# The first branch's products move into the second attention; four more gates become pairs of seven products

## The chip, the cores and the metric

The kernel runs on one core of a Trainium2 chip. The metric is device time in microseconds (us) of one execution. The core's engines are TensorE (PE; PEld is its weight load), VectorE (DVE), ScalarE (ACT), GpSimd (POOL) and SyncE (SP), which issues most DMAs. Each engine works through its own queue in a fixed order and waits on semaphores of the others.

## The reference

One layer of a decoder trunk with 1024 positions and 1024 channels, in float32. Two attentions work on the same normalised input; each goes through a projection (a branch), is weighted by a sigmoid gate, and the sum is mixed and added to x. A gated MLP with a causal convolution follows.

```python
xn = rmsnorm(x, norm_mix_w[l])
proj = xn @ w_in[l]
da_q, da_k, da_v, sw_q, sw_k, sw_v, g_da, g_sw = split_cols(proj)
y_da = diff_attention(da_q, da_k, da_v, lam, lam_init, subln_w[l])     # 4 heads of 128
y_sw = sliding_window_attention(sw_q, sw_k, sw_v, sinks[l])            # 8 heads of 64, window 128
merged = jax.nn.sigmoid(g_da) * (y_da @ w_br_da[l]) + jax.nn.sigmoid(g_sw) * (y_sw @ w_br_sw[l])
x = x + merged @ w_mix_out[l]
x = x + conv_ffn(rmsnorm(x, norm_ffn_w[l]), w_up[l], conv_w[l], conv_b[l], w_down[l])
return rmsnorm(x, norm_final_w)
```

The projection has 34 column blocks of 128: 0 to 17 are the attentions' operands, 18 to 25 the gates of the first branch, 26 to 33 those of the second.

## The kernel before, in words

Activations lie transposed, channels on the 128 partitions and the 1024 positions along the free axis, in halves of 512. Each float32 operand is kept as a high part (a rounded cast, ACT) and a low part (the rest, a subtraction), and each product is three matmuls: high by high, high by low, low by high (`mm3`, lines 146 to 155, and `product`, line 879). A column block with 1024 input rows is 8 x 3 x 2 = 48 matmuls of 512 columns.

**Projections** (`project`). x is split into `xh` and `xl`, eight tiles each, and stays in the chip. Blocks 0, 4, 8, 18 and 20 (`plain`) are computed with 48 matmuls each. The others in `pairs` are computed two at a time by seven products instead of eight (a scheme of Strassen's kind): four input blocks, 7 x 4 x 3 = 84 matmuls for two column blocks; sums of weights are made on POOL (lines 97 to 100), splits on ACT and DVE (lines 111 and 113), and `recombine` (lines 440 to 453) adds the seven products on DVE. Operands of the attentions are then multiplied by `rstd` on POOL (line 436) and stored; gates (18 to 22) are stored in DRAM (`gd`) as they are, without `rstd` and without sigmoid.

**Attentions** (`attention`). Six units: four heads of the first attention (units 0 to 3), two groups of the second (units 4 and 5), eight steps each. The second one's step is `sw_step`: scores on PE, bias and row minimum on DVE (line 714), exponentials on ACT (line 716), scaling, transposes, and products with v. Two small POOL instructions per step (lines 711 and 719) write the sink's column. The remaining eleven gates, 23 to 33, are the background: `back_half` computes one half of a gate in 24 matmuls into a bank of `psG` (two banks), copies it on ACT (line 548) and stores it. The table `HALVES` says after which step each half is issued: two ahead of unit 0, two or three per unit 0 to 3, four in unit 4, three in unit 5, four in the lead-in to the branches. The scheduler orders each engine's queue by that program order, but takes a later instruction first when the earlier ones aren't ready in its own model of time, so background lies between the steps' matmuls singly and in small groups. A head's result is normalised over the next unit's first steps (`da_norm`, line 678 is its last pass) and stored (`yd`).

**Branches** (`rest`). The eight parts of y are loaded (line 763, four buffers `yr`) and split into `yh` and `yl` (lines 806 and 807), with the last four background halves between them. Then the loop at line 770 goes over the eight column blocks: two gates are loaded, multiplied by `rstd` on POOL (line 776) and passed through the sigmoid on ACT (line 783); first branch, 24 matmuls into `sc`; second branch, 24 into `g`; DVE multiplies each with its gate (lines 787 and 792), POOL adds them (line 793), and the sum is split (lines 796 and 797) for the mixing product (`mix`), which leaves the last block for the end of its first product.

**MLP** (`hidden`, `down`). In `down`, four column blocks at lines 1105 to 1114 run while `sums_h` (line 992) prepares the next stage's operands.

Weights come through `next_w`, two ahead: load on SP, cast on ACT (line 132), low part on DVE (line 134).

## Time and profile before

| | before |
|---|---|
| median of 3 runs | 1345.0 us (1343.14 to 1346.02) |
| profiled execution | 1344.88 us, span 1343.0 us |
| mean granted PE clock | 0.997 |
| PE / DVE / ACT / POOL busy | 99 / 78 / 45 / 36% of the span |

| stage | us from the span's start |
|---|---|
| first blocks, plain gates | 0 to 66 |
| nine pairs of seven products | 66 to 237 |
| attentions with eleven background gates | 237 to 488 |
| lead-in: last background, y loaded and split | 488 to 502 |
| both branches and the gates | 502 to 589 |
| mixing product | 589 to 677 |
| MLP | 677 to 1343 |

A line of the groups gives source line, engine, operation, tiles (out<-in), shape and count, then busy time, mean ns of one, and idle time ahead of them with what ended it. A row of windows gives a stretch, its length and each engine's busy time with the count of instructions, the granted PE clock, and the DMA engines' share and rate. A row of the timeline or of the chain of waits gives start, length, and what ran. A DMA row gives size and median time from issue to landing. Matmul lengths overlap; the time from one start to the next is what counts.

### The profile page before, as it was taken

How to read it: one execution, taken by the hardware profiler on the slowest of the kernel's cores; microseconds unless marked ns; L12 is line 12 of the kernel's file. 1: busy time of each engine (PE TensorE's matmuls, PEld its weight loads, DVE VectorE, ACT ScalarE, POOL GpSimd, SP SyncE). 2: the span in 40 equal slices, each digit the busy share in tenths (PEclk: the TensorE clock that was granted, in tenths of full speed). 3: DMA queues.
4: the chain of work that ended last, by engine and by line, in shares of the span. 5: the costliest groups of instructions: out<-in, count | busy, mean ns of one | idle time of the engine just before them, and what ended most of it. 6: DMA issues, size and time to landing. Idle time of an engine off the chain costs nothing.

```text
span 1343.0 us, 17167 instructions
## 1 busy us (share of the span) xinstructions
PE 1326.8 (99%) x6304; PEld 1105.7 (82%) x6304; DVE 1052.5 (78%) x1425; ACT 602.3 (45%) x929; POOL 488.8 (36%) x364
## 2 busy tenths in 40 slices
PE   8999999999999999999999999999999999999997
PEld 6888888888888878888888888888888888788886
DVE  7846775388898976445669999999999998967454
ACT  8432232276667774344444434343434345432433
POOL 0346652000101016642446566666666611131011
PEclk9999999999999999999999999999999999999998
DMA  7244443966554245324522222222222239642342
GB/s 258 108 146 162 148 149 119 273 170 189 143 148 144 70 155 206 141 95 130 167 79 95 79 79 85 88 79 79 88 85 80 86 128 320 220 145 98 94 141 79
DMA packets 63812, 179.49 MB, mean 134 GB/s; under 512 B 7024, under 2 KB 16880, under 8 KB 63728
## 3 DMA queue, kind: packets, MB, share of 16 engines
q1 hardware_dynamic: 52272, 161.22, 36.8%
q10 hardware_dynamic: 11456, 17.18, 3.5%
q8 instruction: 50, 0.82, 0.2%
q14 instruction: 34, 0.28, 0.1%
HBM read 129.61 MB, written 48.76 MB: 133 GB/s over the span
## 4 chain that ended last, share of the span: by engine, by line
PE 72%; DVE 15%; issue 8%; DMA 2%; ACT 1%; POOL 1%; SPq 0%; POOLq 0%; DVEq 0%; ACTq 0%
PE t L887 24%; PE g L153 4%; PE g L154 4%; PE g L155 4%; DVE c L1031 3%; PE y L1056 3%; PE d L1056 3%; PE sc L154 3%; PE sc L155 3%; PE sc L153 3%; PE d L887 3%; PE sc L619 3%; PE y L887 2%; DVE wl L113 2%; DMA hr<-hd 2%
## 5 line engine op out<-in xcount | busy, mean ns | idle before, releaser
L1020 POOL TENSOR_TENSOR us<-us,rstd 128x1024 f32<-128x1024 f32 x42 | 92.6, 2225 | 85.0 <-DVE us L452 47.6
L1029 ACT ACTIVATE c<-us,vecs 128x1024 f32<-128x1024 f32 x44 | 54.8, 1248 | 118.3 <-POOL us L1020 113.8
L132 ACT CAST wh<-raw 128x1024 fp32r<-128x1024 f32 (+2 forms) x58 | 58.7, 1012 | 107.9 <-PE sc L154 35.8
L134 DVE TENSOR_TENSOR wl<-raw,wh 128x1024 fp32r<-128x1024 f32 (+2 forms) x58 | 78.3, 1352 | 32.5 <-ACT wh L132 22.8
L113 DVE TENSOR_TENSOR sl<-sf,sh 128x1024 fp32r<-128x1024 f32 x62 | 89.3, 1442 | 12.8 <-ACT sh L111 12.8
L111 ACT CAST sh<-sf 128x1024 fp32r<-128x1024 f32 x62 | 64.5, 1042 | 61.6 <-PE t L887 44.0
L97 POOL TENSOR_TENSOR sf<-rv 128x512 f32<-128x512 f32 x30 | 51.3, 1711 | 93.6 <-DVE sl L113 51.1
L1031 DVE SCALAR_TENSOR_TENSOR c<-us,vecs,c 128x1024 f32<-128x1024 f32 x44 | 75.4, 1746 | 2.7 <-ACT c L1029 2.7
L99 POOL TENSOR_TENSOR sf<-raw,rv 128x512 f32<-128x512 f32 x30 | 56.7, 1891 | 46.3 <-DVE sl L113 46.3
L1032 DVE SCALAR_TENSOR_TENSOR c<-us,vecs,c 128x1024 f32<-128x1024 f32 x44 | 73.2, 1696 | 0.0
L153 PE MATMUL g<-xh,wh 128*128 128x512 f32 x176 | 71.0, 403 | 1.5 <-ACT g L548 1.5
L154 PE MATMUL g<-xl,wh 128*128 128x512 f32 x176 | 70.3, 400 | 0.0
L155 PE MATMUL g<-xh,wl 128*128 128x512 f32 x176 | 70.3, 399 | 0.0
L170 POOL TENSOR_TENSOR rs<-ms,mhalf 128x8 f32<-128x8 f32 (+2 forms) x9 | 13.5, 1499 | 155.5 <-DVE ms L168 149.4
L1012 ACT ACTIVATE c<-c 128x1024 f32<-128x1024 f32 x22 | 23.4, 1064 | 89.6 <-DVE c L1032 89.6
L113 DVE TENSOR_TENSOR wl<-raw,wh 128x1024 fp32r<-128x1024 f32 (+1 forms) x35 | 61.8, 1765 | 0.3 <-ACT wh L111 0.2
L602 POOL MEMSET aT<- 128x128 f32 x32 | 6.1, 204 | 151.5 <-PE t L648 101.2
L623 DVE CUSTOM_DVE_ANT_0 L<-sc,bias 128x128 f32<-128x128 f32 (+7 forms) x64 | 47.8, 752 | 16.6 <-PE sc L619 13.7
L98 POOL TENSOR_TENSOR sf<-sf,raw 128x512 f32<-128x512 f32 x31 | 58.2, 1877 | 2.2
L624 ACT ACTIVATE L<-L,sm 128x128 f32<-128x128 f32 (+7 forms) x64 | 49.6, 778 | 20.0 <-DVE sm L623 17.3
L776 POOL TENSOR_TENSOR gr<-gr,rstd 128x1024 f32<-128x1024 f32 x16 | 40.3, 2523 | 43.9 <-DMA gr<-gd 43.7
L113 DVE TENSOR_TENSOR wl<-rv,wh 128x512 fp32r<-128x512 f32 x30 | 54.0, 1800 | 2.6 <-ACT wh L111 2.6
(435 smaller groups left out, 4338.4 us busy)
## 6 DMA issues: line engine op xcount, KB each, us to landing
u<-qd SPq DMA_DIRECT2D x72, 256.0 KB, 6.4
raw<-in_w_down SPq DMA_DIRECT2D x27, 512.0 KB, 3.7
hr<-hd SPq DMA_DIRECT2D x50, 256.0 KB, 4.8
raw<-in_w_up SPq DMA_DIRECT2D x23, 512.0 KB, 3.5
raw<-in_w_in SPq DMA_DIRECT2D x22, 512.0 KB, 3.8
hd<-c SPq DMA_DIRECT2D x22, 512.0 KB, 2.6
rv<-in_w_up SPq DMA_DIRECT2D x21, 512.0 KB, 3.5
gr<-gd SPq DMA_DIRECT2D x16, 512.0 KB, 3.4
```

The source lines that it names most:

```text
L111: cast = nc.scalar.copy(hi, src)
L113: low = nc.vector.tensor_tensor(lo, src, hi.bitcast(F32), ALU.subtract)
L132: self.hi = nc.scalar.copy(wh, raw)
L134: self.lo = (eng or nc.vector).tensor_tensor(wl, raw, wh.bitcast(F32), ALU.subtract)
L153: nc.tensor.matmul(ps, wh[:, kc + o, :], ah, start=first and n == 0, stop=False)
L154: nc.tensor.matmul(ps, wh[:, kc + o, :], al, start=False, stop=False)
L155: nc.tensor.matmul(ps, wl[:, kc + o, :], ah, start=False, stop=last and n == len(kcs) - 1)
L887: nc.tensor.matmul(ps, (ah, ah, al)[p][:, k, :], (bh, bl, bh)[p], start=first and n == p == 0, stop=last and p == 2 and n == len(ks) - 1, ...
L1020: i = (nc.vector if m % NF == 0 else nc.gpsimd).tensor_tensor(us[:, 2:], us[:, 2:], self.rstd, ALU.mult)
L1031: nc.vector.scalar_tensor_tensor(c, us[:, 1:T + 1], cw[1], c, ALU.mult, ALU.add)
L1032: nc.vector.scalar_tensor_tensor(c, us[:, 0:T], cw[0], c, ALU.mult, ALU.add)
L1056: nc.tensor.matmul(ps, v[:, n, :], x, start=n == i == 0, stop=n == len(js) - 1 and i == 2)
```

## The change

- Gates 23 to 26 leave the background and become two more pairs, (23, 24) and (25, 26). Seven gates, 27 to 33, stay there.
- Gates computed in the projections (18 to 26) are finished there: times `rstd` (on DVE for the plain ones, POOL for the pairs), sigmoid on ACT, and then stored.
- The first branch leaves `rest`. It becomes background in the second attention and the lead-in, sixteen halves of 12 matmuls (`back_work`): nine from step 5 of unit 4 on, seven in the lead-in. At step 2 of unit 4 heads 0 and 1 are loaded again; heads 2 and 3 are still in the chip and are no longer stored. Ahead of the first half `first_branch` splits the four heads into the tiles of x's first four blocks (low parts in turn on DVE and POOL). Each half is copied from its bank by ACT and multiplied by its finished gate on POOL, into tiles of x's other blocks (`r1`).
- `rest` loads and splits only the second attention's four parts, and its loop computes only the second branch: gate, 24 matmuls, product with the gate on DVE, the sum with `r1` on DVE, split into x's tiles again. Gate 26 needs no `rstd` and sigmoid there.
- The branch weights come in two halves, first the rows of the first branch and then the others, two column blocks per load.
- In `down` each of the four `sums_h` comes behind `next_w` of its block, its instructions on ACT behind the weights' cast; before, the first came at the end of the loop ahead and the others behind the products.

```diff
-HALVES = ((2,), (0, 0, 0, 0, 1, 0, 1, 0), (0, 0, 0, 0, 1, 0, 1, 0), (0, 0, 0, 0, 1, 0, 1, 0), (0, 0, 0, 1, 1, 0, 1, 0), (1, 0, 1, 0, 1, 0, 1, 0), (0, 0, 1, 0, 1, 0, 1, 0), (4,))
+HALVES = ((2,), (0, 0, 0, 0, 1, 0, 1, 0), (0, 0, 0, 0, 1, 0, 1, 0), (0, 0, 0, 0, 1, 0, 1, 0),
+          (0, 0, 0, 1, 1, 0, 1, 1), (0, 1, 0, 1, 0, 1, 0, 1), (1, 1, 1, 1, 1, 1, 1, 0), (7,))
...
-        self.pairs = [(1, 5), (9, 2), (6, 10), (3, 7), (11, 12), (13, 16), (17, 14), (15, 19), (21, 22)]
-        gates = list(range(23, 34))
+        self.pairs = [(1, 5), (9, 2), (6, 10), (3, 7), (11, 12), (13, 16), (17, 14), (15, 19), (21, 22), (23, 24), (25, 26)]
+        gates = list(range(27, 34))
...
-        todo = [(m, hf) for m in gates for hf in range(2)]
+        todo = [(m, hf) for m in gates for hf in range(2)] + [(m, hf) for m in range(KC) for hf in range(2)]
...
-        src += [(self.w_br[m], KC) for m in range(KC)]
+        src += [(self.w_br[m:m + 2, :, o:o + 4, :].rearrange("m p k c -> p m k c"), KC) for o in (0, 4) for m in range(0, KC, 2)]
...
-                    nc.scalar.copy(g, p)
+                    nc.vector.tensor_tensor(g, p, self.rstd[:, hf * H2:(hf + 1) * H2], ALU.mult)
+                    nc.scalar.activation(g, g, AF.Sigmoid)
                     nc.scalar.dma_start(self.gd[m - 18, :, hf * H2:(hf + 1) * H2], g)
...
+                    nc.gpsimd.tensor_tensor(u, u, self.rstd, ALU.mult)
                     if self.kind[m] == "g":
+                        nc.scalar.activation(u, u, AF.Sigmoid)
                         nc.sync.dma_start(self.gd[m - 18], u)
                     else:
-                        nc.gpsimd.tensor_tensor(u, u, self.rstd, ALU.mult)
                         self.keep(m, u, (tp, "hi"))
...
+                    if (u, i) == (4, 2):
+                        raws = [self.tl(self.fpool, [P, T], "f", bufs=2) for _ in range(2)] + ys
+                        for c in range(2):
+                            nc.sync.dma_start(raws[c], self.yd[c])
                     for b in self.back[u + 1][i]:
-                        self.back_half(*b)
+                        if b == (0, 0):
+                            self.first_branch(raws)
+                        self.back_work(*b)
...
+    def first_branch(self, raws):
+        nc = self.nc
+        self.y1 = [self.split(*(self.tl(self.xp, [P, T], f"x{2 * c + p}", F32R) for p in range(2)), r, nc.gpsimd if c % 2 else nc.vector) for c, r in enumerate(raws)]
+        self.r1 = []
+
+    def back_work(self, m, hf):
+        nc = self.nc
+        if m < KC:
+            if hf == 0:
+                if m % 2 == 0:
+                    self.pw = self.next_w()
+                self.g1 = self.tl(self.fpool, [P, T], "fy"[m % 2], bufs=2)
+                nc.sync.dma_start(self.g1, self.gd[m])
+                self.r1.append(self.tl(self.xp, [P, T], f"x{KC + m}"))
+            cols = slice(hf * H2, (hf + 1) * H2)
+            ps = self.tl(self.psG, [P, H2], "g")
+            self.mm3(ps, self.pw, lambda kc, h: [t[:, h * H2:(h + 1) * H2] for t in self.y1[kc]], hf, range(4), o=m % 2 * 4)
+            r = self.r1[m][:, cols]
+            nc.scalar.copy(r, ps)
+            nc.gpsimd.tensor_tensor(r, r, self.g1[:, cols], ALU.mult)
+            return
...
-            if hf == 1:
+            if hf == 1 and h < 2:
                 self.store(self.yd[h], y)
...
-                for c in range(8):
+                for c in range(4, 8):
...
                 for m in range(KC):
-                    w = self.next_w()
...
+                    if m % 2 == 0:
+                        w = self.next_w()
+                    g = self.tl(bp, [P, T], "gr", bufs=4)
+                    nc.sync.dma_start(g, self.gd[8 + m])
+                    if m:
                         i = nc.gpsimd.tensor_tensor(g, g, self.rstd, ALU.mult)
...
                     ps = self.tl(self.psS, [P, T], "sc")
-                    self.mm3_both(ps, w, yact[0], range(4))
-                    nc.vector.tensor_tensor(gs[0], gs[0], ps, ALU.mult)
...
-                    (nc.vector if m == KC - 1 else nc.gpsimd).tensor_tensor(gs[0], gs[0], gs[1], ALU.add)
-                    a = mp.tile([P, T], F32R, name=f"mh{m}")
-                    b = mp.tile([P, T], F32R, name=f"ml{m}")
-                    nc.scalar.copy(a, gs[0])
-                    nc.vector.tensor_tensor(b, gs[0], a.bitcast(F32), ALU.subtract)
+                    self.mm3_both(ps, w, yact, range(4), o=m % 2 * 4)
+                    nc.vector.tensor_tensor(g, g, ps, ALU.mult)
+                    nc.vector.tensor_tensor(g, self.r1[m], g, ALU.add)
+                    a, b = (self.tl(self.xp, [P, T], f"x{k}", F32R) for k in (m, KC + m))
+                    self.split(a, b, g)
...
-                if i == len(self.pieces) - 1:
-                    sums.pop(0)()
...
                 wh, wl = self.next_w()
+                with tc.issue_after(self.hi.ins):
+                    sums.pop(0)()
...
-                if sums:
-                    sums.pop(0)()
```

38 lines of the change are left out of this document (13 added, 25 removed).

## The prediction

> **What bounds the kernel now.** I read the page first, then the stages, then the chain of waits, and last the stretch in which the change puts its new background work.
>
> ```profile
> span 1343.0 us, 17167 instructions
> PE 1326.8 (99%) x6304; PEld 1105.7 (82%) x6304; DVE 1052.5 (78%) x1425; ACT 602.3 (45%) x929; POOL 488.8 (36%) x364
> ```
>
> ```profile
> core 0: us, PE busy (x) PEld busy (x) DVE busy (x) ACT busy (x) POOL busy (x), PEclk, DMA share, GB/s
> 66.00:237.00 171.00, 171.00 (x756) 141.61 (x755) 112.22 (x115) 49.71 (x59) 84.53 (x48) 1.00 0.40 147
> 421.00:455.00 34.00, 33.82 (x203) 28.81 (x202) 32.01 (x109) 26.26 (x75) 3.02 (x12) 1.00 0.45 144
> 455.00:488.00 33.00, 31.40 (x167) 25.13 (x166) 29.33 (x92) 22.94 (x62) 1.67 (x7) 1.00 0.31 96
> 488.00:508.00 20.00, 20.00 (x90) 16.57 (x89) 12.79 (x12) 15.49 (x18) 6.14 (x3) 1.00 0.68 247
> 508.00:590.00 82.00, 82.00 (x364) 67.91 (x363) 41.31 (x36) 29.81 (x30) 56.56 (x21) 1.00 0.40 147
> ```
>
> The windows are the nine pairs of the projections, the second half of the attention (two rows), the lead-in to the branch products and the branch products. PE has something in hand everywhere: time is the sum of PE's work plus a few short holes. So a removed matmul is worth its issue time, as long as PE has another one ready. The exception is the second attention: there DVE is busy 32.01 of 34 and 29.33 of 33 us, and PE is full only because gate products fill the places between attention steps. The chain of waits gives the issue time, and the groups by line the counts (the three lines 153 to 155 have the same count each):
>
> ```profile
> 66.32 171.36 PE t L887 x756
> ```
>
> ```profile
> L153 PE MATMUL g<-xh,wh 128*128 128x512 f32 x176 | 71.0, 403 | 1.5 <-ACT g L548 1.5
> L153 PE MATMUL sc<-yh,wh 128*128 128x512 f32 x64 | 24.9, 389 | 0.0
> L153 PE MATMUL g<-yh,wh 128*128 128x512 f32 x64 | 24.9, 389 | 0.0
> ```
>
> 171.36 / 756 = 0.2267 us per 512-column matmul (the 389 to 403 ns are lengths that overlap). 3 x 176 = 528 matmuls are the eleven background gates, 48 each; 756 / 9 = 84 are a pair of seven products; 3 x 64 = 192 are each branch.
>
> **Part 1, four gates in two pairs.** 4 x 48 = 192 matmuls go, 2 x 84 = 168 come: 24 fewer, 24 x 0.2267 = **-5.4 us**. The first branch's 192 matmuls only move, and replace the 192 of those gates as background; background plus first branch fall from 528 + 192 to 336 + 192.
>
> **Part 2, side work in the projections: 0.** A pair lasts 84 x 0.2267 = 19.0 us on PE. DVE has 112.22 / 9 = 12.5 us of work per pair there.
>
> ```profile
> L436 POOL TENSOR_TENSOR us<-us,rstd 128x1024 f32<-128x1024 f32 x15 | 39.7, 2650 | 13.9 <-DVE us L452 13.8
> L783 ACT ACTIVATE gr<-gr 128x1024 f32<-128x1024 f32 x16 | 17.0, 1061 | 34.0 <-POOL gr L776 34.0
> L447 DVE TENSOR_TENSOR us<-t,s 128x512 f32<-128x512 f32 x31 | 21.1, 681 | 5.2 <-issue 5.2
> gd<-us SPq DMA_DIRECT2D x3, 512.0 KB, 4.4
> 497.82 1.28 ACT L783 ACT_TABLE_LOAD   x1
> ```
>
> POOL has 84.53 / 9 = 9.4 us per pair; a gate tile now adds 2.65 on POOL and 1.06 on ACT, as attention tiles already do with more behind them. Each gate's store waits 3.7 us longer on SP, the last one as the attention's loads begin; if these stood behind it, they would start 3.7 us later. Cover: the two halves of gate 27 and their successors, 48 matmuls or 10.9 us. The four halves of the plain gates cost DVE 0.68 us each instead of a copy on ACT, behind products that run without a hole. ACT also changes its table twice more, 1.28 us each, in a stage of 171 us with ACT 49.71 busy. Without these covers it would be 3.7 + 2.6 = 6.3 us, the other end; I take 0, since products run through both places without a hole.
>
> **Part 3, the hand-over from gates to first branch.** Here the change adds a wait. The matmuls into the background's banks, by stretch:
>
> ```profile
> core 0: us, PE busy (x), PEclk, DMA share, GB/s
> 237.40:421.05 183.65, 93.00 (x336) 1.00 0.64 172
> 421.05:434.00 12.95, 7.21 (x25) 1.00 0.73 243
> 434.00:487.60 53.60, 30.87 (x103) 1.00 0.29 91
> 487.60:502.45 14.85, 14.78 (x66) 1.00 0.55 188
> ```
>
> ```profile
> 421.05:434.00 12.95, 12.77 (x78) 10.79 (x77) 12.19 (x38) 10.14 (x27) 1.79 (x4) 1.00 0.73 243
> 421.06 0.75 DVE L678 SCALAR_TENSOR_TENSOR y<-y,subw,t 128x512 f32<-128x512 f32 x1
> L806 ACT CAST yh<-yr 128x1024 fp32r<-128x1024 f32 x8 | 8.2, 1048 | 1.7 <-DMA yr<-yd 1.7
> L807 DVE TENSOR_TENSOR yl<-yr,yh 128x1024 fp32r<-128x1024 f32 x8 | 9.5, 1220 | 3.4 <-ACT yh L806 3.4
> L776 POOL TENSOR_TENSOR gr<-gr,rstd 128x1024 f32<-128x1024 f32 x16 | 40.3, 2523 | 43.9 <-DMA gr<-gd 43.7
> ```
>
> By 421.05 the kernel before has used 336 = 14 x 24 gate matmuls, exactly what the new kernel has in all. The next background needs the first branch's operands. They overwrite parts of x that the last gate reads, so they can't be made earlier, and head 3 is only finished at 421.06 + 0.75 = 421.8. Four casts of 1.05 then stand on ACT, two subtractions of 1.22 on DVE, two on POOL (price of a two-input pass: 2.52). From 421.05 to 434 PE spent 25 x 0.2267 = 5.7 of 12.95 us on background, 44%. Without background that share is lost, since the steps themselves are held by DVE (12.19 of 12.95). Lower end: products follow the parts one by one from 423 on: 2 us dry, 0.9 lost. Upper end: the casts only get ACT's free share (10.14 of 12.95 is taken, 22% is free): 4.2 / 0.22 = 19 us, less the first part's 3 us, 16 us dry, 7 lost. The casts are queued in program order ahead of the next steps' exponentials, which is nearer the lower end: cast and subtracted by 426.5, 5.5 us dry, **+2.4 us**.
>
> **Part 4, more work beside the attention's steps: 0 on the path.** DVE gains 2 x 1.22, ACT 4.2, POOL two subtractions and nine half-width multiplies (2.52 / 2 = 1.26 each). The attention's last step slips by 2.4 us (DVE alone) to 6.6 (DVE and ACT one after the other). Eight gate loads and two of the heads move here too, onto SP; the DMA engines are 0.45 and 0.31 busy in the two windows above, where the loads of the attention's next operands also stand. The first gate load waits until a head's buffer is split; behind it on SP stand weights and key loads, which are needed one step later or more. Behind the last step comes the second branch:
>
> ```profile
> 489.63 0.39 ACTq L540 DMA_DIRECT2D yd<-ys  x1
> 496.01 3.73 SPq L763 DMA_DIRECT2D yr<-yd  x4
> ```
>
> ```profile
> yr<-yd SPq DMA_DIRECT2D x8, 512.0 KB, 5.0
> yd<-ys ACTq DMA_DIRECT2D x16, 128.0 KB, 1.9
> ```
>
> The last store is issued at 489.63 and lands 1.9 later; its load takes 5.0 (0.5 more for the second of the two), cast and subtraction 2.3: ready at 499.3. Before, those four loads stood until 496.01 because all four buffers held the first branch; now they have the buffers for themselves. PE would need the last part at 502.45 (66 background matmuls after 487.6) plus ten matmuls, 504.7. Margin 5.4 us, plus the 2.4 us by which Part 3 delays PE: 7.8, against a slip of up to 6.6.
>
> **Part 5, the merging loop: 0.** A column block of the second branch is 24 matmuls, 5.44 us, where it was 10.9 for both.
>
> ```profile
> L787 DVE TENSOR_TENSOR gr<-gr,sc 128x1024 f32<-128x1024 f32 x7 | 8.5, 1214 | 0.0
> L797 DVE TENSOR_TENSOR ml<-gr,mh 128x1024 fp32r<-128x1024 f32 x7 | 8.6, 1226 | 20.2 <-ACT mh L796 20.2
> L134 DVE TENSOR_TENSOR wl<-raw,wh 128x1024 fp32r<-128x1024 f32 x8 | 16.8, 2099 | 14.0 <-ACT wh L132 14.0
> ```
>
> DVE per block: product 1.21, sum 1.22, low part 1.23, half a weight split 0.6 to 1.05: 4.3 to 4.7. ACT 1.06 + 1.05 + 0.5; POOL 2.52. All below 5.44. The last block's 1.21 + 1.22 + 1.05 + 1.23 = 4.7 us hide under the mixing product's 42 early matmuls, 9.5 us.
>
> The Trainium skill, "SBUF — State Buffer", section "Who interferes with whom", says that a DVE instruction with two SBUF inputs contends with a GpSimd instruction that reads SBUF, and that whoever starts first blocks the other entirely. The trace agrees in one row, the weight split at 2.10 here; the low part's 1.23 shows no such wait. By that rule every sum, low part and weight split could stand behind a 2.52 us POOL pass; the third rival below has the time.
>
> **Part 6, the sums in the down projection.** The weights' cast now comes ahead of the sums' casts:
>
> ```profile
> 1167.08 2.40 ACT L806 CAST h<-hr 128x512 fp32r<-128x512 f32 x4 [4.48 <-DVE hr L999]
> 1169.39 1.04 ACT L132 CAST wh<-raw 128x1024 fp32r<-128x1024 f32 x1
> 1170.48 2.11 PE L887 MATMUL y<-h,wh 128*128 128x512 f32 x8 [0.30 <-ACT wh L132]
> 1173.05 1.20 PE L887 MATMUL y<-h,wl 128*128 128x512 f32 x4 [0.45 <-DVE wl L134]
> ```
>
> From the rows, 0.30 + 0.45 us of idle, up to 1.1 by the starts (1169.79 + 0.23 to 1170.48, and 1173.05 against 1170.48 + 8 x 0.2267). The last sums come one weight load later, with 24 matmuls (5.4 us) in front of them. **-0.8 us**, between -1.1 and 0.
>
> **Part 7, finer background.** Background now comes in pieces of 12 (2.7 us) with two banks, and PE's queue is in order, so a late copy holds it sooner; eight fewer stores on ACT work the other way. PE's holes from 421 to 488 are 0.18 + 1.60. Between -1 and +3; **+0.5**.
>
> **Sum.** -5.4 + 2.4 - 0.8 + 0.5 = -3.3. The profiled execution took 1344.88 us (span 1343.0 plus 1.9), 0.1 below the median of 1345.0: 1341.6, say **1341.7 us**; its own range is 1339.5 to 1342.3.
>
> **The rivals.** A measurement of this kernel tells about 0.2%, 2.7 us: below 1342.3 is faster, above 1347.7 slower.
>
> 1. The hand-over is long: the casts wait in ACT's gaps, 16 us dry. Loss 7 instead of 2.4: +1.3, about 1346. For it: ACT is 78% taken and PE reads all four parts in every product. Against it: program order. 0.24.
> 2. Nothing is lost: parts come one by one, all holes shrink: -5.4 + 0.9 - 1.1 - 1 = -6.6, about 1338. 0.10.
> 3. DVE becomes the bound of the merging loop, the other side. If a block costs DVE d us, the loss is 8 x (d - 5.44) less the 4.8 us of spare cover (9.5 - 4.7). With sum, low part and half a split each one POOL pass later, d reaches 4.3 + 2.5 x 1.2 = 7.3 (a whole pass costs at most what the split shows, 2.10 against 1.2, and a little more): loss 10, about 1352; at d = 6.2, a loss of 1.3, 1343. It ends slower once d passes 6.8. Against it: L797's 1.226. 0.10.
> 4. POOL's new passes hold the steps: the small POOL copies that each step needs queue behind 9 x 1.26 + 2 x 2.52 = 16 us. A slip of 16 is 8.2 beyond the margin: about 1350; slower from a slip of 13.8. 0.09.
>
> **How the numbers follow.** Forecast 0.47; it and the second rival are faster: 0.57. Rival 1 is the band within 0.2%: 0.24. Rivals 3 and 4: 0.19. The range 1338 to 1348, whose top is the forecast plus Part 2's 6.3, leaves out the lower part of rival 2 (0.04) and most of the slower cases (0.16).
>
> **What would show it.** PE with 24 matmuls fewer and the projections 38 us longer; a stretch near 421 + 38 = 459 without background, some 5 us; the four loads of the second branch issued at once when the last store lands; the merging loop at 5.44 us per block without holes; no hole at the sums. The prediction is wrong if background stays away over 15 us, if PE waits for DVE in the merging loop, or if the second branch's operands arrive after the last background matmul.

## The result and the profile after

The changed kernel takes 1355.7 us (median of 4 runs, 1353.8 to 1357.3) against 1345.4 for the kernel before on the same chip: 1.0079 times as long, 95% interval 1.006 to 1.0098, slower by some 10.3 us. Forecast were 1341.7 us, with 1348 as the top of the range. The profiled execution took 1354.8 us.

The page of the changed kernel:

```profile
span 1353.0 us, 17176 instructions
PE 1325.8 (98%) x6280; PEld 1100.8 (81%) x6280; DVE 1078.3 (80%) x1436; ACT 612.9 (45%) x945; POOL 501.0 (37%) x381
```

PE has exactly the 24 matmuls fewer of Part 1, and the span is 10.0 us longer. (PE's busy time falls by 1.0 only: the lengths of matmuls overlap, those around a wait are longer, and the mean granted clock is 0.994 to 0.996 in its four runs after 0.997 or 0.998 in the kernel before; more in the last section.) So the question is where PE stands still. The windows of the changed kernel, stage by stage (length, then busy time of PE, PEld, DVE, ACT, POOL with instruction counts, the granted clock, DMA share and rate):

```profile
core 0: us, PE busy (x) PEld busy (x) DVE busy (x) ACT busy (x) POOL busy (x), PEclk, DMA share, GB/s
66.00:275.00 209.00, 209.00 (x924) 173.06 (x923) 139.04 (x139) 65.48 (x75) 109.80 (x61) 1.00 0.40 143
275.20:297.90 22.70, 20.99 (x98) 17.18 (x96) 5.67 (x9) 8.13 (x11) 4.04 (x7) 1.00 0.73 218
434.00:455.00 21.00, 20.97 (x150) 19.20 (x150) 17.19 (x61) 15.36 (x44) 3.22 (x10) 1.00 0.66 155
455.00:476.50 21.50, 15.24 (x84) 12.16 (x83) 19.84 (x52) 15.59 (x37) 5.53 (x7) 0.86 0.27 86
476.50:542.60 66.10, 62.70 (x342) 51.31 (x341) 60.29 (x184) 47.33 (x129) 17.57 (x29) 0.99 0.34 107
542.60:553.90 11.30, 11.30 (x51) 9.35 (x50) 4.15 (x5) 5.42 (x9) 5.38 (x4) 1.00 0.65 224
553.90:597.40 43.50, 42.41 (x184) 33.99 (x183) 34.62 (x25) 20.98 (x21) 21.61 (x8) 1.00 0.48 170
```

The eleven pairs run without a hole. PE then misses 1.7 us ahead of the first score (297.9), 6.3 us from 455.0 to 476.5 and 3.4 us in the rest of the second attention, nothing in the lead-in, and 1.1 us in the merging loop. Of the background alone (matmuls into the two `g` banks; length, PE's busy time, clock, DMA), in the changed kernel:

```profile
275.20:434.00 158.80, 80.68 (x305) 1.00 0.64 173
434.00:455.00 21.00, 8.46 (x32) 1.00 0.66 155
455.00:476.50 21.50, 0.86 (x3) 0.86 0.27 86
476.50:542.60 66.10, 40.44 (x142) 0.99 0.34 107
```

By 455 the 336 gate matmuls are used: the last one starts at 454.98. Of the first branch, one matmul runs at 461.87, from high parts alone; the second, which needs a low part, starts at 476.55:

```profile
461.87 0.50 PE L155 MATMUL g<-x,wh 128*128 128x512 f32 x1 [1.02 <-ACT g L584]
476.55 0.63 PE L156 MATMUL g<-x,wh 128*128 128x512 f32 x1
```

That is a stretch of 21.5 us, dry but for one matmul, where 5.5 were forecast. Two places lead to it.

**The last pair.** The queues after the last pair's products (275.2), first SP, then ACT and DVE:

```profile
279.07 1.94 SPq L439 DMA_DIRECT2D gd<-us  x2
282.89 0.33 SPq L124 DMA_DIRECT2D raw<-in_w_in  x1
284.86 1.13 SPq L595 DMA_DIRECT2D u<-qd  x2
```

```profile
276.69 1.28 ACT L438 ACT_TABLE_LOAD   x1
277.99 1.06 ACT L438 ACTIVATE us<-us 128x1024 f32<-128x1024 f32 x1
279.61 1.06 ACT L438 ACTIVATE us<-us 128x1024 f32<-128x1024 f32 x1 [0.56 <-POOL us L436]
280.57 1.03 ACT L134 CAST wh<-raw 128x1024 fp32r<-128x1024 f32 x1
```

```profile
281.64 1.23 DVE L136 TENSOR_TENSOR wl<-raw,wh 128x1024 fp32r<-128x1024 f32 x1 [4.35 <-ACT wh L134]
```

The two stores stand on SP ahead of the attention's loads and wait for POOL's scale, the table load and the sigmoids. The weight load behind them waits for DVE's low part at 281.64 to read the buffer that it needs; that follows the cast at 280.57, which stands behind the sigmoids on ACT. So the first `u` load is issued 9.7 us after the last pair's product instead of 3.6 (240.90 in the kernel before), and the first score comes 22.7 us after it instead of 18.1.

**The hand-over.** The changed kernel's timeline: POOL, then DVE, then PE.

```profile
465.66 2.38 POOL L835 TENSOR_TENSOR x<-f,x 128x1024 fp32r<-128x1024 f32 x1 [0.79 <-ACT x L834]
468.49 2.42 POOL L835 TENSOR_TENSOR x<-y,x 128x1024 fp32r<-128x1024 f32 x1
```

```profile
465.94 0.75 DVE L714 SCALAR_TENSOR_TENSOR y<-y,subw,t 128x512 f32<-128x512 f32 x1 [0.26 <-PE t L178]
467.48 3.58 DVE L757 TENSOR_SCALAR L<-L,sw 128x255 f32<-128x255 f32 x4
472.98 1.22 DVE L835 TENSOR_TENSOR x<-f,x 128x1024 fp32r<-128x1024 f32 x1
476.54 1.22 DVE L835 TENSOR_TENSOR x<-y,x 128x1024 fp32r<-128x1024 f32 x1
```

```profile
472.11 2.07 PE L774 MATMUL t<-aT,v 128*128 128x512 f32 x4 [3.89 <-DVE aT L768]
```

Line 714 is the last pass on head 3: the last operand is finished at 466.7, 32.7 us after the second attention's first score at 434.0. In the kernel before it was 32.6 us (389.2 to 421.8). But the stock of gate matmuls is gone earlier: the last of the 336 starts 21.0 us after that score, in the kernel before 31.6. So 11.7 of the 21.5 us pass before the last head can be split at all, and 9.8 behind that.

In those 9.8 us, four row scalings took 3.58 us, where four take 1.36 in the kernel before: one of them took 2.43 and ended just after POOL's pass, which ends at 470.91. DVE's own two low parts come behind those scalings and the rest of a step, at 472.98 and 476.54, some 7 us after POOL began the first.

### The profile page after: what moved, and what is told of

Same layout as the page of the kernel before. It is cut to its first block, busy times and chain, and to the rows that moved or that the text cites. A ratio compares the mean times of both kernels' runs of the same rounds, so it can differ in the third digit from the quotient of the medians.

```text
span 1353.0 us, 17176 instructions
## 1 busy us (share of the span) xinstructions
PE 1325.8 (98%) x6280; PEld 1100.8 (81%) x6280; DVE 1078.3 (80%) x1436; ACT 612.9 (45%) x945; POOL 501.0 (37%) x381
## 4 chain that ended last, share of the span: by engine, by line
PE 90%; DVE 5%; issue 2%; DMA 1%; ACT 1%; SPq 0%; POOL 0%; POOLq 0%; DVEq 0%; ACTq 0%
PE t L915 46%; PE y L1084 3%; PE d L1084 3%; PE sc L655 3%; PE sc L155 3%; PE sc L156 2%; PE sc L157 2%; PE d L1111 2%; PE y L1111 2%; PE g L156 2%; PE g L157 2%; PE d L915 2%; PE g L155 2%; PE y L915 2%; PE t L671 1%
## 5 line engine op out<-in xcount | busy, mean ns | idle before, releaser
L1048 POOL TENSOR_TENSOR us<-us,rstd 128x1024 f32<-128x1024 f32 x42 | 93.0, 2233 | 84.9 <-DVE us L456 48.1
L115 DVE TENSOR_TENSOR sl<-sf,sh 128x1024 fp32r<-128x1024 f32 x66 | 98.3, 1490 | 11.6 <-ACT sh L113 11.6
L134 ACT CAST wh<-raw 128x1024 fp32r<-128x1024 f32 (+2 forms) x54 | 54.6, 1010 | 108.0 <-PE sc L156 33.5
L113 ACT CAST sh<-sf 128x1024 fp32r<-128x1024 f32 x66 | 68.7, 1043 | 69.1 <-PE t L915 51.4
L99 POOL TENSOR_TENSOR sf<-rv 128x512 f32<-128x512 f32 x32 | 54.6, 1705 | 106.2 <-DVE sl L115 57.2
L136 DVE TENSOR_TENSOR wl<-raw,wh 128x1024 fp32r<-128x1024 f32 (+2 forms) x54 | 66.9, 1241 | 25.0 <-ACT wh L134 20.5
L155 PE MATMUL g<-x,wh 128*128 128x512 f32 x176 | 69.9, 398 | 1.0 <-ACT g L584 1.0
L157 PE MATMUL g<-x,wl 128*128 128x512 f32 x176 | 70.6, 401 | 0.0
L156 PE MATMUL g<-x,wh 128*128 128x512 f32 x176 | 70.2, 399 | 0.0
L436 POOL TENSOR_TENSOR us<-us,rstd 128x1024 f32<-128x1024 f32 x22 | 57.3, 2608 | 30.9 <-DVE us L456 15.8
L115 DVE TENSOR_TENSOR wl<-rv,wh 128x512 fp32r<-128x512 f32 x32 | 57.1, 1786 | 2.6 <-ACT wh L113 2.6
L915 PE MATMUL t<-x,wh 128*128 128x512 f32 x176 | 54.2, 389 | 0.0
```

Of the source, the lines that this page charges most:

```text
L113: cast = nc.scalar.copy(hi, src)
L115: low = nc.vector.tensor_tensor(lo, src, hi.bitcast(F32), ALU.subtract)
L136: self.lo = (eng or nc.vector).tensor_tensor(wl, raw, wh.bitcast(F32), ALU.subtract)
L155: nc.tensor.matmul(ps, wh[:, kc + o, :], ah, start=first and n == 0, stop=False)
L156: nc.tensor.matmul(ps, wh[:, kc + o, :], al, start=False, stop=False)
L157: nc.tensor.matmul(ps, wl[:, kc + o, :], ah, start=False, stop=last and n == len(kcs) - 1)
```

## The experiments

Each time is a median; differences are to the changed kernel's 1355.7 unless another is named, and the kernel before, run beside each group, stood between 1344.7 and 1346.1. Stretches of A+ count from the last pair's last product.

### One cause at a time

Gates 25 and 26 stored unfinished:

```diff
-                    nc.gpsimd.tensor_tensor(u, u, self.rstd, ALU.mult)
+                    if m < 25:
+                        nc.gpsimd.tensor_tensor(u, u, self.rstd, ALU.mult)
                     if self.kind[m] == "g":
-                        nc.scalar.activation(u, u, AF.Sigmoid)
+                        if m < 25:
+                            nc.scalar.activation(u, u, AF.Sigmoid)
```

> The changed kernel, but the last pair's two gates (25, 26) are stored as they come from the recombination, without the multiplication by rstd on POOL and the sigmoid on ACT (left out altogether, so blocks 25 and 26 are weighted with raw gates). Theory A (the attention's first loads stand on SP behind the finished gates' stores): the first score matmul comes 18 us after the last pair's last matmul again (22.7 in the changed kernel), and the whole is 4 to 5 us shorter than the changed kernel, about 1351. Theory B (POOL's new passes in the second attention hold DVE): no more than 1 us, 1355. Theory C (the hand-over between gates and first branch is the loss, and loads are covered by background): no more than 1 us, 1355.

Measured 1349.1 us (1.0027 times before, 1.0013 to 1.004), 6.6 us less. The first score comes at A+19.0. Only 1.7 us of this was PE's own hole ahead of the first score. More came from the background, here up to the second attention's first score in this run:

```profile
275.20:429.00 153.80, 78.04 (x290) 1.00 0.65 180
```

290 gate matmuls are used by then, 305 in the changed kernel. The cover did hide the wait, but 15 matmuls (3.4 us) that it spent were missing at the hand-over: the stock now lasts until 27.0 us after the second attention's first score instead of 21.0. The lower clock of the changed kernel is gone as well (0.997 or 0.998 in all seven runs), so not all of the 6.6 us is the stock's.

The last pair's stores on ACT's queue, still finished:

```diff
-                        nc.sync.dma_start(self.gd[m - 18], u)
+                        (nc.scalar if m > 24 else nc.sync).dma_start(self.gd[m - 18], u)
```

> The changed kernel with all its work; only the stores of gates 25 and 26 are issued from ACT's queue instead of SP's, so that SP has nothing to wait for ahead of the attention's loads. Theory A: as with the raw pair, the first score matmul at about 18 us after the last pair and 3 to 5 us shorter, about 1352. Theories B and C: within 1 us of the changed kernel.

1352.9 us (1.0062, 1.0047 to 1.0077): 2.8 less, with the first score at A+21.3. The stores' place on SP is 2.8 of the 6.6 us. SP now issues three of the attention's first four loads by 275.2, but the fourth only at 282.0, after a wait of 6.7 us that the profile puts down to the gates' stores, which ACT issues behind the sigmoids. PE has no hole of its own ahead of this first score.

The first branch's low parts all on DVE, its gate product on DVE from the bank, without ACT's copy and POOL:

```diff
-... self.split(..., r, nc.gpsimd if c % 2 else nc.vector) for c, r in enumerate(raws)]
+... self.split(..., r) for c, r in enumerate(raws)]
...
-            nc.scalar.copy(r, ps)
-            nc.gpsimd.tensor_tensor(r, r, self.g1[:, cols], ALU.mult)
+            nc.vector.tensor_tensor(r, ps, self.g1[:, cols], ALU.mult)
```

> The changed kernel, but the first branch uses POOL for nothing: the four low parts are all made on DVE, and each half's product is multiplied by its gate on DVE straight from PSUM (no copy on ACT). DVE gets 2 x 1.2 + 9 x 0.7 = 8.7 us more in the second attention, POOL's 4.8 + 12 us go. Theory B (POOL's passes lock DVE out: the row scaling took 24.7 us instead of 18.5): the scaling is back at 341 ns each and the whole is 6 us or more shorter, under 1350. Theory C: the hand-over stays (its first product still comes after four splits), 0 to 3 us shorter or longer, 1353 to 1358. Theory A: the same as C.

1358.4 us (1.0109, 1.0087 to 1.013): 2.7 more. Row scalings are back at 341 ns, but DVE took the removed work: 11 products of 0.68 us and two more low parts in the window, which then has DVE busy 99.8 us instead of 97.3. Moving POOL's work to DVE pays back nothing.

The first branch with x's own parts as operands, no fetch and no splits:

```diff
-        self.y1 = [self.split(*(self.tl(self.xp, [P, T], f"x{2 * c + p}", F32R) ...) for c, r in enumerate(raws)]
+        self.y1 = [(self.xh[c], self.xl[c]) for c in range(4)]
```

> The changed kernel, but the first branch's products read the parts of x's first four blocks that are in the chip all the time; the heads are not loaded again and not split (left out, so the first branch is computed from the wrong operand). PE's work is the same and nothing is to be waited for. Theory C: the stretch of 21 us without background (455 to 476) is gone and the whole is 8 to 12 us shorter than the changed kernel, 1344 to 1348. Theory A: no more than 2 us shorter, 1354. Theory B: 2 to 4 us shorter (two of POOL's passes go).

1351.2 us (1.0054, 1.0037 to 1.0071): 4.5 less, under the expected 8 to 12. The background of this run in the stretch that was dry:

```profile
455.00:476.50 21.50, 8.72 (x29) 1.00 0.33 95
```

29 matmuls instead of 3, but the steps' own waits stay.

Both left out:

> Leaves out both the row norm's scale and the sigmoid of gates 25 and 26 (stored as they are), and the fetch and split of the second attention's first two heads (the first branch multiplies the parts that x has already), so the computation is not the reference's; it says whether the two costs are separate. Alone the first was worth 6.6 us against the changed kernel and the second 4.5. If the late start and the dry stretch are two costs, they add: 1355.7 - 11.1 = 1344.6, within 2 us. If both are the same cost seen twice (the attention steps run late, and whatever starts them earlier removes the same stalls), the sum is not more than the larger: about 1349. The stalls from 450 to 500 us are then what tells: under the first they fall to under 5 us in all.

1345.7 us (1.0007, 0.9997 to 1.0016), 10.0 less; the two alone make 11.1. They nearly add, but not cleanly: each alone also ends the lower clock, which can go only once, and PE's waits for DVE's product in the merging loop rise from 1.1 us in the changed kernel to 2.2. Some 6 us remain above the kernel before less the two terms that came true (1345.4, less 5.4 for the matmuls and 0.4 measured at the sums, makes 1339.6).

### What remains: POOL's passes

From that kernel, the product of the first branch with its gate left out:

```diff
-            nc.gpsimd.tensor_tensor(r, r, self.g1[:, cols], ALU.mult)
```

> As the run that left out the last pair's finishing and the heads' fetch and splits (1345.7), and the product of the first branch with its gate is left out too (16 passes of 1.3 to 1.4 us on POOL), so nothing of this change runs on POOL beside the second attention. If POOL's passes cost there: row scalings at 341 ns, stalls of 500 to 550 us from 5.5 to 2 to 3, 1342 to 1344. If the steps' own chains cost: 1345.7, within 1 us.

1343.1 us (0.9987, 0.9976 to 0.9999), 2.6 less than 1345.7. The row scaling in the kernel before, the changed one, the run at 1345.7, and this one:

```profile
L721 DVE TENSOR_SCALAR L<-L,sw 128x255 f32<-128x255 f32 (+1 forms) x64 | 18.5, 341 | 0.4
```

```profile
L757 DVE TENSOR_SCALAR L<-L,sw 128x255 f32<-128x255 f32 (+1 forms) x64 | 24.7, 441 | 0.3
```

```profile
L757 DVE TENSOR_SCALAR L<-L,sw 128x255 f32<-128x255 f32 (+1 forms) x64 | 21.3, 381 | 0.4
```

```profile
L756 DVE TENSOR_SCALAR L<-L,sw 128x255 f32<-128x255 f32 (+1 forms) x64 | 18.6, 340 | 0.4
```

The gate product is worth 41 ns per scaling, 64 times: 2.6 us of DVE. The other 60 of the changed kernel's 100 ns had gone with the last pair and the splits. PE's wait for the scalings (1.6 us from 400 to 600 us in the run at 1345.7) is gone too.

Then also the merging loop's scale by `rstd` on POOL left out:

```diff
                     if m:
-                        i = nc.gpsimd.tensor_tensor(g, g, self.rstd, ALU.mult)
                         with tc.issue_after(self.hi.ins):
                             nc.scalar.activation(g, g, AF.Sigmoid)
```

> As the run before, and the row norm's scale on the seven gates of the merging loop is left out (seven POOL passes of 2.4 us). If they hold the loop's VectorE: the stalls of 1.2 to 1.4 us at the bank hand-over go and the stalls from 550 to 600 us (3.4 us) fall under 1: 1339.5 to 1342, the sum of the forecast without any of its losses. If VectorE's own chain is too long for the loop: no change within 0.7 us.

1339.2 us (0.9957, 0.994 to 0.9974), 3.9 less again, and 0.4 from 1339.6. The account closes within the noise of the medians (the interval of this ratio alone is 4.6 us wide). The merging loop's DVE groups, in the changed kernel, in the run at 1345.7 and in this one:

```profile
L835 DVE TENSOR_TENSOR x<-gr,x 128x1024 fp32r<-128x1024 f32 x8 | 13.8, 1720 | 6.7 <-ACT x L834 6.7
```

```profile
L835 DVE TENSOR_TENSOR x<-gr,x 128x1024 fp32r<-128x1024 f32 x8 | 16.1, 2013 | 6.7 <-ACT x L834 6.7
L823 DVE TENSOR_TENSOR gr<-x,gr 128x1024 f32<-128x1024 f32 x8 | 11.9, 1483 | 0.3
```

```profile
L830 DVE TENSOR_TENSOR x<-gr,x 128x1024 fp32r<-128x1024 f32 x8 | 9.8, 1225 | 6.7 <-ACT x L829 6.7
L818 DVE TENSOR_TENSOR gr<-x,gr 128x1024 f32<-128x1024 f32 x8 | 9.8, 1222 | 0.1
```

The low part costs 1.72 and 2.01 us beside POOL and 1.23 without. The waits of PE for DVE's product from 538 to 620 us, in the run at 1345.7 and in the one at 1343.1 (total, times, longest):

```profile
PE sc L155 <- DVE gr L821: 2.2, 2, 1.1
```

```profile
PE sc L155 <- DVE gr L820: 2.9, 3, 1.2
```

PE waits for a bank that DVE's product has yet to read, and the product stands behind the held low part. In the last run no such line is left: 2.9 of the 3.9 us are this wait.

### Repairs

Gates 25 and 26 finished where they are used, 25 in the lead-in, 26 in the merging loop:

```diff
                 nc.sync.dma_start(self.g1, self.gd[m])
+                if m == 7:
+                    i = nc.gpsimd.tensor_tensor(self.g1, self.g1, self.rstd, ALU.mult)
+                    ...
+                    nc.scalar.activation(self.g1, self.g1, AF.Sigmoid)
...
-                    if m:
+                    if True:
```

> The whole computation. The last pair's two gates are stored as they are, and scale and sigmoid of gate 25 are made where it is used (the last first-branch product), those of gate 26 in the merging loop like the other plain gates'. If the late start of the attention comes from the finishing of the last pair on SP's, POOL's and ScalarE's way, and the finishing itself is cheap elsewhere, this takes the time of the run that left it out: 1349, within 2 us, with the first score at A+19 (A: last pair product). If POOL's pass (2.4 us) and the sigmoid amid the second attention's steps cost as much as they saved, it stays at 1353 to 1357.

1350.0 us (1.0039, 1.0024 to 1.0054): 5.7 less, the best of the repairs, and still slower than the kernel before.

The same with `first_branch` at a higher rank:

```diff
-                            self.first_branch(raws)
+                            with tc.high_priority(200):
+                                self.first_branch(raws)
```

> As the run with the late finish, and the first branch (its fetch and splits first) gets a higher rank in the order of the engines' queues, so that VectorE's low parts stand ahead of the spread of row scalings they stood behind. If the dry stretch at the hand-over is a matter of place in VectorE's queue, the second attention's steps get background earlier and up to 4.5 us more go: 1344.5 to 1348. If it is the fetch of the heads and the casts that are late (the data is there only when the first attention's last steps are written), the rank changes nothing: 1349, within 1.5 us. If the rank puts work that must wait ahead of the attention's steps, it is slower than 1350.

1355.1 us (1.0078, 1.0061 to 1.0095), 5.1 more than without: the third case of its expectation. From 466 PE waits 1.7 us with a first-branch matmul that needs POOL's low part of the last head and stands ahead of the steps' matmuls, and the granted clock is halved behind that wait (last section); the rest of the 5.1 was not followed.

And eight gate buffers in the merging loop (`bufs=4` to `bufs=8` for `gr`):

> As the run before, with eight gate buffers in the merging loop instead of four, so that no gate's scaling on POOL has to wait for a buffer. The changed kernel's stalls of 550 to 600 us are 5.0 us in the run that kept x's own parts; the share that comes from VectorE's low parts standing beside POOL's 2.4 us passes is expected to go: 1 to 3 us under the run with the higher rank. If those stalls come from the start of the loop (the late heads' low parts) and not from the gates, no change within 0.7 us.

1358.9 us (1.0101, 1.0086 to 1.0116), 3.8 more: the expectation had the sign wrong. This run's POOL, DVE and PE in the loop:

```profile
554.64 24.39 POOL L819 TENSOR_TENSOR gr<-gr,rstd 128x1024 f32<-128x1024 f32 x8 [3.72 <-DMA gr<-gd]
```

```profile
566.77 3.42 DVE L831 TENSOR_TENSOR gr<-x,gr 128x1024 f32<-128x1024 f32 x1
570.11 3.43 DVE L136 TENSOR_TENSOR wl<-raw,wh 128x1024 fp32r<-128x1024 f32 x1
573.46 3.35 DVE L843 TENSOR_TENSOR x<-gr,x 128x1024 fp32r<-128x1024 f32 x1
```

```profile
578.09 0.77 PE L155 MATMUL sc<-yh,wh 128*128 128x512 f32 x1 [4.66 <-DVE gr L829]
```

With a buffer for each, POOL's eight passes stand end to end for 24 us. DVE's instructions with two SBUF inputs take 2.1 to 3.4 us beside them for 1.22, while its product that reads PSUM (line 829) stays at 1.21. With four buffers only the first four passes stand end to end (10.5 us), the other four apart.

The plain gates' scale put on by DVE as a half leaves its bank, with the late finish:

```diff
-        self.nc.scalar.copy(g, ps)
+        self.nc.vector.tensor_tensor(g, ps, self.rstd[:, hf * H2:(hf + 1) * H2], ALU.mult)
```

> The whole computation. As the run with the late finish (gates 25 and 26 finished at their use), and the row norm's scale of the seven plain gates 27 to 33 is put on by VectorE when the half leaves its bank (one product from PSUM in place of ScalarE's copy), not by POOL in the merging loop, where only gate 26 keeps a POOL pass. Theory (POOL's passes hold VectorE's additions in the merging loop: 2 to 3.4 us for 1.22): the loop's stalls of 1.2 to 1.7 us go, and 2 to 4 us against the 1350.0 of the late finish: 1346 to 1348. Rival (the loop waits for the late heads' parts or for the gate fetch): the same stalls without POOL, 1350. Second rival: the 14 products on VectorE among the attention steps cost as much as they save: 1350 to 1353, and the last score of the first attention comes later than A+152.4.

1357.3 us (1.0082, 1.0067 to 1.0097), 7.3 more than the late finish alone. PE has no wait left in the loop's blocks (560 to 640 us), so that part of the theory held; the second rival decides. The background up to the second attention's first score, in the late finish and in this run:

```profile
275.31:428.31 153.00, 78.01 (x290) 1.00 0.65 180
```

```profile
275.48:433.66 158.18, 83.94 (x315) 1.00 0.65 179
```

The first attention is 5.2 us longer. PE doesn't stand still there; it uses 25 more gate matmuls, which are missing later. The lower clock is back, too (0.994 to 0.996 in its four runs, 0.997 or 0.998 with the late finish).

That drain in the changed kernel alone:

> The changed kernel with the plain gates' scale put on by VectorE as the half leaves its bank; nothing left out. The changed kernel itself shows 2.3 us of stalls from 550 to 600 us, 1.2 of them in the merging loop. Theory: these go and nothing else changes, 1353.5 to 1354.5. Rival: VectorE's 14 products of some 0.65 us (9 us) come between the attention steps, and it is slower, 1356 to 1360.

1355.2 us (1.007, 1.0053 to 1.0087), no change that can be told.

One half of a gate moved from the first attention's last head into the second attention, in the kernel with drain and late finish, and in the changed kernel alone:

```diff
-          (0, 0, 0, 1, 1, 0, 1, 1), (0, 1, 0, 1, 0, 1, 0, 1), (1, 1, 1, 1, 1, 1, 1, 0), (7,))
+          (0, 0, 0, 0, 1, 0, 1, 1), (0, 1, 0, 1, 0, 1, 0, 1), (1, 1, 1, 1, 1, 1, 1, 1), (7,))
```

> As the run before, and one half of a plain gate is moved from the first attention's last head into the second attention's first half (the table of background pieces: the last head's step 3 without one, the first-branch halves one place later, eight steps of the second group with one). If the dry stretch of the hand-over is what costs (about 4.5 us, 24 more matmuls of 0.227 us are there to fill it), 2 to 4.5 us under the run before. If the steps of the second attention wait for their own chain and not for lack of filling, no change within 1 us. If the first attention misses the half, its stalls grow by up to 5 us.

> The changed kernel with the shifted table alone, nothing left out. Background lasts 5.4 us longer into the second attention before the first branch has to be ready. If lack of background at the hand-over is the cost: 1351 to 1353 instead of 1355.7. If it is VectorE's queue blocked behind POOL's passes and the heads' parts: 1355, within 1 us.

1358.5 (1.0091, 1.0076 to 1.0106) and 1355.3 us (1.008, 1.0058 to 1.0102): no gain. In the second, no background runs from 440 to about 460 us instead of from 455 to 476. This one placement moved the gap and didn't close it; others weren't tried.

### A theory that fell: DVE's time bounds the second attention

In the kernel before, the changed one and the twelve of the first three groups of runs DVE is busy 88 to 93% of the second attention, whether it lasts 98 or 113 us. That looks like a bound. Two of four row scalings left out:

```diff
-        for h in range(4):
+        for h in range(2):
             self.last = nc.vector.tensor_scalar(L[:, h, a:w], L[:, h, a:w], s[:, 3, h:h + 1], None, ALU.mult)
```

> The changed kernel, with the row scaling of two of the four heads left out in each step of the second attention (the rows stay unnormed): 32 of 64 row scalings of 441 ns, 12.4 us of VectorE's 97.3 us in the window, 85 left. If VectorE's time is the bound, the window from first score to last product goes from 108.6 to 85 / 0.9 = 94 us, unless TensorE's 98.9 us of work there (less what background then is left for after it) holds it at 97 to 100: 8 to 12 us under the changed kernel, 1344 to 1348. If the chain of a step with too little background is the bound, the scaling's share of the chain goes, 2 of 4 scalings or 0.9 us in some steps, and the window stays above 104: 1351 to 1355.

1352.9 us (1.0058, 1.004 to 1.0076), 2.7 less. Its window:

```profile
433.50:534.20 100.70, 93.91 (x556) 77.30 (x555) 87.53 (x263) 76.96 (x207) 27.22 (x45) 1.00 0.44 130
```

The attention is 7.9 us shorter than the 108.6 of the changed kernel, but 16 matmuls fewer ran in it (556 for 572), and they come after it; a part of the 5.0 us by which PE's busy time fell is the clock, 1.00 here and 0.97 there. A stage can shorten by more than the time does, since PE's idle time counts, not the stage's length.

The same 32 scalings on ACT (`nc.scalar.mul` for heads 2 and 3), in the changed kernel, with the late finish, and in the kernel before:

> The changed kernel, the same 32 scalings done by ScalarE (a copy with a factor), nothing left out. VectorE 85 us, ScalarE 78.3 + 32 x about 0.4 to 0.5 us = 91 to 94 us in the window. If VectorE's time is the bound: the window goes to 100 to 104 (ScalarE is now as loaded as VectorE), 4 to 8 us under the changed kernel, 1348 to 1352. If the chain is the bound, ScalarE's scalings stand behind exponentials of the same step and it is slower than 1355.7.

> The late finish of the last pair (1350.0) and the 32 scalings on ScalarE together; the whole computation. If the costs are separate: 1350.0 less 4 to 8 us, 1342 to 1346, at or below the kernel before (1345). If the chain is the bound: 1350 or slower.

> The kernel before with the 32 scalings on ScalarE; the whole computation. VectorE 89.5 - 32 x 0.341 = 78.6 us in the window of 98.3 us, ScalarE 71.6 + 13 to 16 = 85 to 88. TensorE is busy there 96.3 of 98.3 us, so at most the 3 to 5 us of stalls from 400 to 500 us can go: 1340 to 1344 if VectorE bounds the window in the kernel before too; 1345, within 1 us, if TensorE does there.

1354.0 (1.0066, 1.0048 to 1.0084), 1352.0 (1.005, 1.0034 to 1.0066) and 1347.4 us (1.0012, 1.0003 to 1.0022). The changed kernel gains 1.7 us at most. Neither the late finish (1350.0) nor the kernel before gains by it; both medians are some 2 us higher, which for the late finish is within the noise. In the kernel before the second attention lasts 100.7 us with DVE busy 81.3 of them, after 98.3 with 89.5: DVE's sum of work isn't the bound there. What limits a step besides was not measured by itself. None of the repairs beats the kernel before.

## Why the prediction was wrong

**Part 1 (-5.4): right.** 6304 - 6280 = 24, and the pairs end 37.9 us later, where 2 x 84 x 0.2267 = 38.1 was due.

**Part 2 (0): the first failed step.** The place and the other end, 6.3, were named; leaving the last pair's finishing out measured 6.6. The attention's first loads came 6.1 us later (9.7 after 3.6), where 3.7 were reckoned. What failed is "products run through both places without a hole". They nearly did (1.7 us), but the cover was the same stock of 336 matmuls that Part 3 counted as spent by the hand-over: 15 of them went here. A delay ahead of a shortage isn't hidden by spending the stock. That leaving the finishing out gives nearly the 6.3 of the other end is chance: that figure had neither the stock nor the clock in it.

**Part 3 (+2.4): right in mechanism, too small.** The stretch was 21.5 us, beyond even the 16 us of the first rival, yet without the splits only 4.5 us go. Two steps failed. The stock was taken to last until head 3 is finished, as in the kernel before ("exactly what the new kernel has in all"). It was gone 11.7 us ahead of that; of the 10.6 us by which it ended sooner after the second attention's first score, 6.0 are Part 2's delay (21.0, 27.0 without the last pair's finishing, 31.6 before), and the rest was not traced. And the 4.7 us from head 3 to the split operands (421.8 to 426.5) were 9.8. There it was "queued in program order ahead of the next steps' exponentials" that failed: casts and low parts lay between the instructions of later steps, DVE's two low parts behind row scalings that POOL's low part held.

**Part 4 (0): wrong, by another way than was weighed.** The second branch's operands were in time: the lead-in has no hole, so the margin held. But POOL's gate products slow the row scalings, by 41 ns each where the rest is repaired, and 2.6 us go with them; that DVE's own instructions get longer beside POOL was no term of the sum. The fourth rival named these passes and the steps as their victim, but with POOL's own queue as the way.

**Part 5 (0): wrong, as the third rival said.** The Trainium skill's rule ("SBUF — State Buffer", "Who interferes with whom") was set against one row of 1.23 us and lost; that row came from a loop of 10.9 us per block, where POOL's passes and the low parts seem to have missed each other. In the new loop the low part takes 1.72 us in the changed kernel and up to 3.4 in a run with POOL's passes end to end, and the rule holds. Its price is 3.9 us where the rest is repaired, not the rival's 10. In the changed kernel itself PE waits only 1.1 us in the loop; the wait grows to 2.9 as the stages ahead of it get faster. That a whole pass costs at most what the split shows (2.10 against 1.2) was wrong in the third rival: 3.43 against 1.22 was seen.

**Part 6 (-0.8): half.** The two waits at the sums are gone; from the first matmul of the MLP to the last it is 659.8 us after 660.2, -0.4, in one profiled execution of each. In the changed kernel:

```profile
1175.60 1.98 PE L915 MATMUL y<-h,wh 128*128 128x512 f32 x8
1177.41 0.84 PE L915 MATMUL y<-h,wl 128*128 128x512 f32 x3
```

**Part 7 (+0.5):** not measured by itself. The others leave little room for it: -5.4 + 10.0 + 2.6 + 3.9 - 0.4 = 10.7 against 10.3 measured, each cost taken in the order of the runs and each known to about 1 us.

**The rivals.** Each gave one loss with all others at zero. The first (1346), third (1352) and fourth (1350) each had hold of a real cost; none had them together, and the top of the range was the forecast with Part 2's 6.3 alone. In this kernel they came together: Parts 2 and 3 drew on the same stock of background, and Parts 3, 4 and 5 had POOL's passes beside DVE's instructions.

## What to carry to other kernels

Background that fills an in-order engine's holes is a stock: a wait that it hides early is paid where the stock runs out, so follow the count of what is left across stages before calling a delay covered. Work given to an engine that is mostly idle (POOL, 37%) isn't free if it holds another engine's instructions; price each pass by what it can hold. When a loop is made twice as tight, a row from the slack loop is no evidence on contention in the tight one.

## What the runs showed of the hardware

A row scaling with a single SBUF tensor input (128x255, fp32, a factor per row) is held by POOL's passes: 341 ns without, 441 ns in the mean beside them in the changed kernel, and four in 3.58 us when one falls on a pass of 2.4 us. The Trainium skill, "SBUF — State Buffer", section "Who interferes with whom", lists `tensor_scalar` among the instructions that can, where their operands meet its conditions, enter a mode with both port pairs and then contend with GpSimd. The trace agrees that it contends; which mode the scaling ran in, no trace here shows. Against instructions with two SBUF inputs, the wait grows with POOL's density: 1.22 us alone, 1.7 to 2.0 in the mean with four buffers, up to 3.4 with passes end to end.

A wait of PE costs more than its length. Windows of the changed kernel around its longest hole, the 3.89 us quoted at the hand-over:

```profile
468.00:472.00 4.00, 0.22 (x3) 0.00 (x0) 4.00 (x8) 1.71 (x5) 2.60 (x3) 0.79 0.59 171
472.00:476.50 4.50, 4.39 (x16) 3.90 (x17) 3.59 (x8) 1.93 (x5) 0.00 (x0) 0.50 0.35 127
476.50:480.00 3.50, 3.50 (x18) 2.92 (x17) 3.44 (x7) 1.01 (x3) 0.56 (x2) 0.90 1.08 268
```

PE works again from 472 on, at half the granted clock until 476.5 and beyond (1.00 from 477.5 on). An estimate from these rows: 0.50 x 4.5 + 0.10 x 3.5 = 2.6 us of work lost behind the hole. The kernel before has 1.00 in all its windows of that stage. The Trainium skill, "TensorE: Matmul & The Clock Gate", Part 1, says that the clock is halved after an idle window of about 3.4 us and comes back after as long a busy one. The traces agree only in part. In the changed kernel the clock falls at about 470.3, some 2 us into the hole, and in the run with the higher rank it is halved behind a hole of 1.71 us. Its matmul behind that hole, and the window that follows:

```profile
467.77 0.80 PE L156 MATMUL g<-x,wh 128*128 128x512 f32 x1 [1.71 <-POOL x L843]
```

```profile
470.00:475.00 5.00, 5.00 (x19) 3.95 (x18) 3.71 (x10) 1.69 (x4) 0.98 (x1) 0.57 0.28 93
```

So a hole well under 3.4 us can do it, in a stretch with other short waits; how much idle time is enough was not measured. The same is seen in the matmul of 0.77 us behind the 4.66 us hole of the run with eight buffers.

The mean granted clock of every run tells where this falls: 0.994 to 0.996 in the changed kernel, 0.997 or 0.998 in the kernel before and in all runs without the last pair's finishing, without the splits, or with the late finish alone, and 0.993 to 0.997 again with the higher rank, with eight buffers, and with DVE's scale on top of the late finish. So a part of what the first group saved, and of what the second lost, is the clock; how much was not measured by itself.
